# Two layers of a decoder trunk on one core: one block of four small experts moved from the fourth place to the last of 14, and the transposes of the first token tiles moved among the values' products

## The chip, the cores and the metric

The kernel runs on one core of one Trainium2 chip. The metric is device time in microseconds (us) from the first to the last instruction of the core, as the median of several executions. The engines are TensorE (PE in the rows; its weight loads PEld), VectorE (DVE), ScalarE (ACT), GpSimd (POOL), and SyncE (SP), which issues the loads.

## The reference

512 tokens of width 1024 go through two layers and a final norm. Per layer:

```
h  = rms_norm(x)                                   # 512 x 1024
q, k, v, cu, cg, ga, gb = split(h @ w_in)          # 512 wide each, ga and gb 1024
A  = mixture of three dilated windows of attention(q, k, v) @ w_attn_out
B  = silu(layer_norm(depthwise_conv31(cu * sigmoid(cg)))) @ w_conv_out
x += (sigmoid(ga) * A + sigmoid(gb) * B) @ w_out
h2 = rms_norm(x)
group = top-1 of 4;  e1, e2 = top-2 of the group's 8 experts
x += sum over the two experts e: gate_e * ((silu(h2 @ Wg[e]) * (h2 @ Wu[e])) @ Wd[e])
x += sigmoid(rms_norm(x) @ w_ple_gate) * (p @ w_ple_proj)
```

Wg[e] and Wu[e] are 1024 x 512, Wd[e] is 512 x 1024, all in float32; there are 32 experts in each layer.

## The kernel before, in words

**Dense parts.** Tokens are handled in 4 tiles of 128. A float32 product is made of three products of halves: each operand is split into a high part (hi) and the rest (lo), and hi·hi, lo·hi and hi·lo are added (lines 313 to 315). The dense weights lie in chunks of 128x1024; `SEQ_CHUNKS` is their order: v0 to v3 (the values), then cu0, cg0 and so on, pg0 to pg7 last (the gate of the per-layer embeddings). `load_chunks` loads a chunk as s_raw on SP (L217). `split_chunks` makes hi on ACT (L235) and lo: of the four v chunks one half on POOL and one on DVE (L238), of most others the whole 128x1024 on POOL (L240). `take(c)` asks for splits up to chunk c + `self.ahead` and loads up to c + `self.look`.

**The opening of layer 0.** `run` loads the four token tiles and the first chunks. Then it takes the tiles t one after another: the sum of squares on ACT, `prep`, which writes s_n (the normed tile, one operation of 128x1024 on DVE) and appends that tile's `split_T` to the list `self.todo`, and `split_chunks`. `split_T` transposes a tile on TensorE (eight transposes, ps_tr<-s_n, L420), copies the result on ACT (s_hTh, L425) and writes the rest on DVE (s_hTl, L427). In this stretch the program's order on DVE, ACT and POOL is kept as written (`Engines`). Rows of helpers have line 103.

**The values' products.** `tokens_b` calls `token_b` once per token tile: 8 steps k of three products each, ps_tb<-s_hi,s_hTh and its two companions, 96 in all. Chunk v0 serves k = 0 and 1, v1 k = 2 and 3, and so on. `value` copies each tile's result and calls the next `split_T` left in the list. Behind the values stand the chunks of z (ps_z), in steps of 24 products with `step_a`.

**The blocks of experts.** Tokens are sorted to experts with slots. The 28 experts after the first four stand in the order of their load, which is known only after routing: `order_experts` ranks them and gives each a base slot. The eight with the fewest tokens are small (32 slots), the others have 64. `BLK` groups the experts in 14 blocks of 128 slots: two of them each, or four small ones. `moe` takes two blocks per round c: gate and up products of both blocks (ps_g, ps_u), down products of the two blocks of the round before (ps_y), transposes (ps_hT), the gather for the next round (ps_xg), and the combine of the round before (ps_c). After the fifth block stands a loop for tokens that found no slot, at which all queues are drained. In rounds 4 and 5 the projections of the embeddings are added (ps_pe). After the last round the down products of blocks 12 and 13 follow, then their combine (L1150), with transposes of x and the products of the gate behind it.

**The loads of experts.** Weights come in 512 KB tiles, 4 per matrix and expert, in a ring of 45 slots (`s4`, L253). `pump` issues them in the order in which the blocks use them: gate and up of two blocks ahead of the down tiles of the two before, the last down tiles ahead of the raw chunks pg0 to pg7 (L217). SP lets at most eight loads be outstanding: a load is issued when the one eight before it has landed.

Of the kernel before, what the change touches and what calls it, by code (L numbers as in the profile page):

```python
# [13 lines left out]
OP = mybir.AluOpType  # L14
# [5 lines left out]
KD = D // P  # L20
H, HD = 8, 64
CW, CK = 512, 31
NG, NPG, NE = 4, 8, 32
# [3 lines left out]
CAP = 64  # L27
GS = 256


NST, NSM = 4, 8
NDY = NE - NST
LD = 4
BLK = ([(2 * i, 2 * i + 1) for i in range(NST // 2)]
       + [tuple(range(NST + 4 * i, NST + 4 * i + 4)) for i in range(NSM // 4)]
       + [(i, i + 1) for i in range(NST + NSM, NE, 2)])
NB = len(BLK)


# [41 lines left out]
AH = 4  # L81
LK = 5, 3
# [82 lines left out]
class Trunk:  # L165
    def __init__(self, ctx, tc, x, pT, wd, wg, wu, wdn, sm, gains, cst, out):
# [19 lines left out]
        for l in range(self.L):  # L186
            gu = [[(l, w, s, h) for w in ("g", "u") for h in range(4) for s in b
                   if n or w == "u" or h < 4 - LATE] for n, b in enumerate(BLK)]
            dn = [[(l, "d", s, h) for h in range(4) for s in b] for b in BLK]
            seq = gu[:2] + dn[:2]  # L190
# [171 lines left out]
                self.done(c)  # L362
        return ps

    def tokens_b(self, cs, src, then):
        for c in cs:
            self.take(c)
        for t in range(NT):
            then(t, self.token_b(cs, src, t))


    def rsqrt(self, y, a, t, steps=3):
# [63 lines left out]
    def run(self):  # L436
        nc = self.nc
        self.layer = 0
        self.lim = NCH - 1
        nc.sync.dma_start(self.x[0], self.dr["x"][0:P])  # L440
        nc.sync.dma_start(self.ident, self.dr["cst"][:, C_ID:C_ID + P])
        gain = self.gain_row(0)
        for t in range(NT):
            if t:
                nc.sync.dma_start(self.x[t], self.dr["x"][t * P:(t + 1) * P])
            self.load_chunks(t)
        self.small(0)
        self.load_chunks(5)
        self.load_c2()
        nc.sync.dma_start(self.c1[:, C_ID + P:], self.dr["cst"][:, C_ID + P:C_N1])  # L450
        self.oneb = self.one.tile([P, P], BF, name="oneb")
        nc.vector.memset(self.oneb, 1.0)
        self.hT = Rows(self.s4, KD, F32R, "hTh"), Rows(self.s4, KD, F32R, "hTl")
        self.todo = []
        self.nc = Engines(self.tc, ("v", "sc", "g"))
        for t in range(NT):
            n = self.s4.get(F32, "n")
            self.prep(t, gain, self.rms(t, n), n)
            if t in (1, 2):
                self.todo.pop(0)()  # L460
            self.split_chunks(t)
        self.nc = nc
        self.s4.free()
        for l in range(self.L):
            self.layer = l
            self.mixer(l)
            self.moe(l)
            self.ple(l)
# [23 lines left out]
    def mixer(self, l):  # L492
        nc = self.nc
        v, act = nc.vector, nc.scalar
        base = l * NCH
        self.look, self.ahead = LK[0], AH
        pos = self.pos = {s: base + i for i, s in enumerate(SEQ_CHUNKS)}
        self.lim = pos["wo7"]
        conv, attn, side = [], [], []
# [5 lines left out]
        def value(t, ps):  # L505
            act.activation(vt(t), ps, AF.Copy)
            self.ps.free()
            if self.todo:
                self.todo.pop(0)()
        self.tokens_b([pos[f"v{i}"] for i in range(4)], self.hT, value)  # L510

        if l:
            self.load_c2()
        self.scale_small(l)
# [234 lines left out]
        for j in range(8):  # L749
# [14 lines left out]
            for h in range(2):  # L764
# [3 lines left out]
                                       op0=OP.mult, op1=OP.subtract)  # L768
# [17 lines left out]
        cs = [pos[f"wo{i}"] for i in range(4, 8)]  # L786
# [148 lines left out]
    def order_experts(self):  # L935

        v = self.nc.vector
        cnt = self.posb[:, 128:160]
        key, rank, small, base, self.cnt, top, rest, bs = (self.lgT[:, 32 * i:32 * i + 32] for i in range(8))
        bs, ss = bs[:, :8], bs[:, 8:16]  # L940
        over = lambda a, n: a.unsqueeze(1).to_broadcast([P, n, 32])
        down = lambda a, n: a.unsqueeze(2).to_broadcast([P, n, 32])

        v.scalar_tensor_tensor(key, cnt, -32.0, self.cc(C_KEY, 32), op0=OP.mult, op1=OP.add)  # L944
        src = key
        for i in range(0, NE, 8):
            v.max(out=top[:, i:i + 8], in_=src)
            if i + 8 < NE:
                v.match_replace(out=rest, in_to_replace=top[:, i:i + 8], in_values=src, imm_value=-1e9)
                src = rest  # L950
        oi = self.tn(NDY, "oi", I32)
        v.tensor_copy(oi, top[:, :NDY])
        v.tensor_scalar(oi, oi, 31, None, op0=OP.bitwise_and)
        self.order, self.order_v = oi, {}
        tmp = self.s2.get(F32, "ord")
        t3 = tmp.bitcast(BF).rearrange("p (a b) -> p a b", b=32)
        v.tensor_tensor(t3, over(key, 32), down(key, 32), op=OP.is_gt)
        v.tensor_reduce(rank, t3, axis=AX.X, op=OP.add)

        v.tensor_scalar(small, rank, float(NSM), 32.0, op0=OP.is_lt, op1=OP.mult)  # L960
        v.scalar_tensor_tensor(base, rank, float(NSM - 1), small, op0=OP.subtract, op1=OP.mult)
        v.scalar_tensor_tensor(base, rank, float(CAP), base, op0=OP.mult, op1=OP.subtract)
        if CAP * NST != CAP // 2 * NSM:
            v.tensor_scalar(base, base, float(CAP * NST - CAP // 2 * NSM), None, op0=OP.add)
        v.tensor_copy(base[:, :NST], self.cc(C_BASE, NST))
        v.tensor_add(self.cnt, cnt, small)
        self.ps.free()
        E8 = self.Ew[:, 0:256].rearrange("p (g e) -> p g e", e=32)
        t8 = tmp[:, 0:256].rearrange("p (g e) -> p g e", e=32)
        for o, a in ((ss, small), (bs, base)):  # L970
            v.tensor_tensor(t8, E8, over(a, 8), op=OP.mult)
            v.tensor_reduce(o, t8, axis=AX.X, op=OP.add)
        v.tensor_add(self.spos8, self.spos8, ss)
        v.tensor_scalar(ss, self.spos8, float(CAP), 4096.0, op0=OP.is_ge, op1=OP.mult)
        v.tensor_add(ss, ss, bs)
        v.tensor_add(self.slots8, self.spos8, ss)
        self.s2.free()
# [58 lines left out]
    def moe(self, l):  # L1036
# [56 lines left out]
        def gate_up(p, xg, w, ps, hs):  # L1093
            m = P // len(BLK[p])
            for h in hs:
                for k in range(2):
                    for i, e in enumerate(BLK[p]):
                        s = (2 * h + k) % 4 * GS + p % 2 * P + i * m
                        pe.matmul(ps[m * i:m * i + m], xg[h // 2][:, s:s + m], self.half_item((l, w, e, h), k),
                                  start=h == 0 and k == 0, stop=h == 3 and k == 1)  # L1100
                for e in BLK[p]:
                    self.item_free((l, w, e, h))
                self.pump(keep=KEEP[self.c])
# [457 lines left out]
```

## Time and profile before

| What | Value |
| --- | --- |
| time, median of 3 runs | 1854.9 us (1853.12 to 1855.19) |
| the profiled execution's own time | 1849.56 us |
| its span | 1847.8 us |
| TensorE busy | 1750.0 us, 95% |
| DVE, ACT, POOL busy | 47%, 29%, 21% |
| mean granted clock of TensorE | 0.987 |
| moved from memory | 474.90 MB, 258 GB/s over the span |

The profile is of one execution, whose own time lies a little below the median of the runs. Busy shares are averages over stages with different limits. The page's slices show DMA rates of 400 to 419 GB/s in the two stretches of the experts' blocks and some 60 to 80 GB/s in much of the rest. In the rows, `ps_...` are tiles of TensorE's accumulator memory, `s_...` tiles of on-chip memory; the tile written stands ahead of the arrow.

### The profile page before, as it was taken

The numbers are of one execution on the slowest core, as the hardware profiler recorded it, in microseconds if no ns is written. First come the engines' busy times: TensorE is split into PE (matmuls) and PEld (weight loads), VectorE is DVE, ScalarE is ACT, GpSimd is POOL, SyncE is SP. The second block draws the span as 40 slices with busy tenths as digits, with TensorE's granted clock in tenths as the row PEclk, the third lists the DMA queues.
The fourth block names the chain that finished last, engine by engine and source line by source line (L and its number), as shares of the span: only waits on it lengthen the run. The fifth ranks groups of instructions, "written<-read, shape, count | busy, mean of one in ns | idle before, by whom it ended". The sixth has DMA issues, their size and how long they took to land.

```text
span 1847.8 us, 24216 instructions
## 1 busy us (share of the span) xinstructions
PE 1750.0 (95%) x8324; PEld 1055.2 (57%) x8324; DVE 871.8 (47%) x2131; ACT 544.6 (29%) x1041; POOL 379.6 (21%) x203
## 2 busy tenths in 40 slices
PE   5999999989889999999999999999989899999997
PEld 4776777753143455454877777777432443455356
DVE  5587864374041343223558777535620331443146
ACT  4355443321011012112634545342110110121045
POOL 3445332410200001000444443242002000010021
PEclk9999999999999999999999999999999999999999
DMA  5212126479999999997241112554899899999941
GB/s 224 84 65 68 58 79 232 145 264 384 419 359 404 419 419 419 416 419 300 86 133 58 60 57 69 180 195 139 307 391 419 341 418 419 419 414 419 419 197 46
DMA packets 133616, 478.66 MB, mean 259 GB/s; under 512 B 14832, under 2 KB 15344, under 8 KB 133488
## 3 DMA queue, kind: packets, MB, share of 16 engines
q1 hardware_dynamic: 133488, 477.06, 66.4%
q8 instruction: 68, 1.11, 0.2%
q14 instruction: 60, 0.49, 0.1%
HBM read 474.90 MB, written 2.10 MB: 258 GB/s over the span
## 4 chain that ended last, share of the span: by engine, by line
PE 62%; DMA 21%; DVE 8%; issue 5%; ACT 2%; POOL 1%; SPq 0%; POOLq 0%; DVEq 0%; ACTq 0%
DMA s_w<-wdn 11%; PE ps_g L103 8%; PE ps_xg L103 6%; PE ps_u L103 6%; PE ps_z L314 5%; PE ps_z L313 5%; PE ps_z L315 5%; PE ps_y L103 5%; DMA s_w<-wu 5%; PE ps_c L103 5%; DMA s_w<-wg 3%; PE ps_tb L313 2%; PE ps_tb L314 2%; PE ps_tb L315 2%; PE ps_S L634 2%
## 5 line engine op out<-in xcount | busy, mean ns | idle before, releaser
L240 POOL TENSOR_TENSOR s_lo<-s_raw,s_hi 128x1024 fp32r<-128x1024 f32 x114 | 274.8, 2422 | 838.2 <-ACT s_hi L235 464.5
L103 PE MATMUL ps_u<-s_w,s_xg 128*64 128x512 f32 (+1 forms) x1024 | 239.0, 595 | 12.2 <-DMA s_w<-wu 11.8
L103 PE MATMUL ps_g<-s_w,s_xg 128*64 128x512 f32 (+1 forms) x1024 | 225.0, 606 | 14.3 <-DMA s_w<-wdn 9.4
L103 PE MATMUL ps_y<-s_w,s_hT 128*64 128x512 f32 (+1 forms) x1024 | 222.9, 601 | 10.7 <-DMA s_w<-wdn 10.4
L314 PE MATMUL ps_z<-s_hTl,s_hi 128*128 128x512 f32 x512 | 203.9, 398 | 0.0
L313 PE MATMUL ps_z<-s_hTh,s_hi 128*128 128x512 f32 x512 | 201.4, 393 | 0.0
L315 PE MATMUL ps_z<-s_hTh,s_lo 128*128 128x512 f32 x512 | 199.8, 390 | 0.0
L103 PEld LDWEIGHTS ps_u<-s_w,s_xg 128*64 128x64 f32 (+1 forms) x1024 | 67.6, 130 | 178.0 <-issue 118.0
L103 PEld LDWEIGHTS ps_y<-s_w,s_hT 128*64 128x64 f32 (+1 forms) x1024 | 69.2, 131 | 161.7 <-issue 114.3
L103 PEld LDWEIGHTS ps_g<-s_w,s_xg 128*64 128x64 f32 (+1 forms) x1024 | 65.1, 132 | 162.0 <-issue 129.0
L526 DVE SCALAR_TENSOR_TENSOR s_acc<-ps_z,smt,s_acc 128x511 f32<-128x511 f32 (+27 forms) x210 | 153.7, 732 | 4.2
L235 ACT ACTIVATE s_hi<-s_raw 128x1024 fp32r<-128x1024 f32 x120 | 125.4, 1056 | 8.8 <-PE ps_wo L314 4.0
L1108 DVE SCALAR_TENSOR_TENSOR s_h<-s_h,ps_g 128x512 f32<-128x512 f32 x28 | 19.2, 687 | 212.0 <-ACT s_h L1107 194.5
L1107 ACT ACTIVATE s_h<-ps_g,rs 128x512 f32<-128x512 f32 x28 | 19.2, 687 | 328.9 <-PE ps_g L103 327.4
L1153 DVE TENSOR_TENSOR s_x<-s_x,ps_c 128x512 f32<-128x512 f32 x112 | 75.2, 685 | 77.1 <-PE ps_c L103 46.1
L314 PEld LDWEIGHTS ps_z<-s_hTl,s_hi 128*128 128x128 f32 x512 | 96.3, 188 | 21.4 <-issue 3.0
L313 PEld LDWEIGHTS ps_z<-s_hTh,s_hi 128*128 128x128 f32 x512 | 96.1, 188 | 21.3 <-issue 1.0
L103 PE MATMUL ps_xg<-s_OH,s_xh 128*128 128x256 f32 x412 | 104.3, 293 | 3.7 <-DVE s_lgT L944 3.7
L315 PEld LDWEIGHTS ps_z<-s_hTh,s_lo 128*128 128x128 f32 x512 | 96.3, 188 | 19.0
L1118 ACT ACTIVATE s_hT<-ps_hT 128x512 f32<-128x512 f32 x28 | 15.4, 596 | 298.8 <-PE ps_hT L103 298.8
L103 PE MATMUL ps_xg<-s_OH,s_xl 128*128 128x256 f32 x412 | 103.1, 290 | 0.0
L1109 DVE TENSOR_TENSOR s_h<-s_h,ps_u 128x512 f32<-128x512 f32 x28 | 19.2, 687 | 155.2 <-PE ps_u L103 155.2
(274 smaller groups left out, 2815.4 us busy)
## 6 DMA issues: line engine op xcount, KB each, us to landing
s_w<-wu SPq DMA_DIRECT2D x256, 512.0 KB, 9.9
s_w<-wdn SPq DMA_DIRECT2D x256, 512.0 KB, 9.9
s_w<-wg SPq DMA_DIRECT2D x248, 512.0 KB, 9.9
s_raw<-wd SPq DMA_DIRECT2D x124, 512.0 KB, 3.3
s_w<-wg SPq DMA_DIRECT2D x16, 256.0 KB, 7.6
s_x<-x SPq DMA_DIRECT2D x4, 512.0 KB, 9.7
out<-s_n SPq DMA_DIRECT2D x8, 256.0 KB, 2.0
s_gain<-gains SPq DMA_DIRECT2D x3, 512.0 KB, 5.1
```

Of the source, the lines that this page charges most:

```text
L103: i = f(*a, **k)
L235: nc.scalar.activation(hi, raw, AF.Copy)
L240: nc.gpsimd.tensor_tensor(lo, raw, hi.bitcast(F32), op=OP.subtract)
L313: mm(out, lh, rh, start=start, stop=False)
L314: mm(out, lh, rl, start=False, stop=False)
L315: mm(out, ll, rh, start=False, stop=stop)
L526: v.scalar_tensor_tensor(o, i, w, o, op0=OP.mult, op1=OP.add)
L634: nc.tensor.matmul(ps[:, off:off + n], qk(0, i * P, (i + 1) * P)[r], qk(1, 0, n)[r], start=True, stop=True)
L1107: act.activation(t, pg, AF.Tanh, scale=rh[p])
L1108: v.scalar_tensor_tensor(t, t, 1.0, pg, op0=OP.add, op1=OP.mult)
L1109: v.tensor_mul(t, t, pu)
L1153: v.tensor_add(xs, xs, ps)
```

## The change

Blocks: `BLK` had two static pairs, two blocks of four small experts (places 2 and 3), ten pairs. It has now two static pairs, one block of four small experts (place 2), ten pairs, and the other block of four small experts at place 13. The rule for the base slot in `order_experts` follows that. Opening: tile 0's `split_T` runs right after its `prep`; the splits of chunks asked for are 0, 2, 3, 3 instead of 0, 1, 2, 3; the other tiles' `split_T` are called, in layer 0, after the fourth of the eight steps k of a values' tile instead of between tiles or ahead of them; and during the values of layer 0 only one chunk is split ahead instead of four.

```
-BLK = ([(2 * i, 2 * i + 1) for i in range(NST // 2)]
-       + [tuple(range(NST + 4 * i, NST + 4 * i + 4)) for i in range(NSM // 4)]
-       + [(i, i + 1) for i in range(NST + NSM, NE, 2)])
+BLK = ([(2 * i, 2 * i + 1) for i in range(NST // 2)] + [tuple(range(NST, NST + 4))]
+       + [(i, i + 1) for i in range(NST + NSM, NE, 2)] + [tuple(range(NST + 4, NST + NSM))])
...
-    def tokens_b(self, cs, src, then):
+    def tokens_b(self, cs, src, then, hook=None):
         for c in cs:
             self.take(c)
         for t in range(NT):
-            then(t, self.token_b(cs, src, t))
+            then(t, self.token_b(cs, src, t, hook))
...
             self.prep(t, gain, self.rms(t, n), n)
-            if t in (1, 2):
+            self.split_chunks((0, 2, 3, 3)[t])
+            if t == 0:
                 self.todo.pop(0)()
-            self.split_chunks(t)
...
-        self.look, self.ahead = LK[0], AH
+        self.look, self.ahead = LK[0], AH if l else 1
...
-            if self.todo:
+            if l and self.todo:
                 self.todo.pop(0)()
-        self.tokens_b([pos[f"v{i}"] for i in range(4)], self.hT, value)
-
+        halves = []
+
+        def middle():
+            halves.append(0)
+            if not l and len(halves) % KD == KD // 2 and self.todo:
+                self.todo.pop(0)()
+        self.tokens_b([pos[f"v{i}"] for i in range(4)], self.hT, value, middle)
+
+        self.ahead = AH
...
-        v.scalar_tensor_tensor(base, rank, float(NSM - 1), small, op0=OP.subtract, op1=OP.mult)
+
+        v.tensor_scalar(bs32, rank, 4.0, -40.0, op0=OP.is_ge, op1=OP.mult)
+        v.scalar_tensor_tensor(bs32, bs32, -11.0, rank, op0=OP.add, op1=OP.add)
+        v.tensor_mul(base, bs32, small)
         v.scalar_tensor_tensor(base, rank, float(CAP), base, op0=OP.mult, op1=OP.subtract)
-        if CAP * NST != CAP // 2 * NSM:
-            v.tensor_scalar(base, base, float(CAP * NST - CAP // 2 * NSM), None, op0=OP.add)
+        v.tensor_scalar(base, base, -128.0, None, op0=OP.add)
```

On TensorE, at the program's start, before: s_n_108 is token tile 0's normed tile, s_n_131 tile 1's; ps_tr holds transposes, ps_tb_260 the first values' tile.

```order
L420 MATMUL ps_tr_149<-c_71,s_n_108 128x128 x4
L420 MATMUL ps_tr_158<-c_71,s_n_108 128x128 x4
L420 MATMUL ps_tr_190<-c_71,s_n_131 128x128 x4
L420 MATMUL ps_tr_199<-c_71,s_n_131 128x128 x4
L313 MATMUL ps_tb_260<-s_hi_126,s_hTh_100 128x512
L314 MATMUL ps_tb_260<-s_lo_127,s_hTh_100 128x512
```

The same engine in the changed kernel, from step k = 3 of the first values' tile (ps_tb_230); the nine products of k = 0 to 2 stand ahead of it, behind tile 0's own eight transposes, and s_n_149 is tile 1's normed tile.

```order
L313 MATMUL ps_tb_230<-s_hi_167,s_hTh_101 128x512
L420 MATMUL ps_tr_243<-c_71,s_n_149 128x128 x4
L420 MATMUL ps_tr_252<-c_71,s_n_149 128x128
L314 MATMUL ps_tb_230<-s_lo_168,s_hTh_101 128x512
L315 MATMUL ps_tb_230<-s_hi_167,s_hTl_105 128x512
L420 MATMUL ps_tr_252<-c_71,s_n_149 128x128 x3
L313 MATMUL ps_tb_230<-s_hi_172,s_hTh_102 128x512
```

Tile 1's transposes moved from ahead of all products to behind the tenth product of tile 0.

On ACT, later in the opening, before: s_hi_231 is the split of chunk 3, the L235 rows with a 128x1024 tile are splits of later chunks, and ps_tr_286 holds transposes of tile 2, ps_tr_330 of tile 3.

```order
L103 ACTIVATE s_hi_231<-s_raw_86 128x1024
L425 ACTIVATE s_hTh_100<-ps_tr_286 128x2x128
L235 ACTIVATE s_hi_238<-s_raw_89 128x1024
L425 ACTIVATE s_hTh_101<-ps_tr_286 128x2x128
L235 ACTIVATE s_hi_242<-s_raw_91 128x1024
L425 ACTIVATE s_hTh_102<-ps_tr_295 128x2x128
L425 ACTIVATE s_hTh_103<-ps_tr_295 128x2x128
L235 ACTIVATE s_hi_248<-s_raw_246 128x1024
L425 ACTIVATE s_hTh_100<-ps_tr_330 128x2x128
```

The same engine in the changed kernel; ps_tr_252 belongs to tile 1, ps_tr_287 and ps_tr_296 to tile 2, and L508 copies a finished values' tile.

```order
L425 ACTIVATE s_hTh_102<-ps_tr_252 128x2x128
L235 ACTIVATE s_hi_224<-s_raw_89 128x1024
L425 ACTIVATE s_hTh_103<-ps_tr_252 128x2x128
L508 ACTIVATE s_v_218<-ps_tb_230 128x512
L425 ACTIVATE s_hTh_100<-ps_tr_287 128x2x128
L425 ACTIVATE s_hTh_101<-ps_tr_287 128x2x128
L425 ACTIVATE s_hTh_102<-ps_tr_296 128x2x128
L425 ACTIVATE s_hTh_103<-ps_tr_296 128x2x128
L508 ACTIVATE s_v_218<-ps_tb_274 128x512
```

One split of a whole chunk (s_raw_89) stands among the copies now; the next two (s_raw_91 and s_raw_246) have moved behind the values.

On TensorE, at the end of layer 0's blocks, before: the last eight down products of block 13 (ps_y, an expert of 64 slots) and the first of the combine (ps_c).

```order
L103 MATMUL ps_y_6559<-s_w_6381,s_hT_6469 64x512
L103 MATMUL ps_y_6559<-s_w_6383,s_hT_6469 64x512
L103 MATMUL ps_y_6560<-s_w_6381,s_hT_6469 64x512
L103 MATMUL ps_y_6560<-s_w_6383,s_hT_6469 64x512
L103 MATMUL ps_y_6559<-s_w_6389,s_hT_6469 64x512
L103 MATMUL ps_y_6559<-s_w_6391,s_hT_6469 64x512
L103 MATMUL ps_y_6560<-s_w_6389,s_hT_6469 64x512
L103 MATMUL ps_y_6560<-s_w_6391,s_hT_6469 64x512
L1150 MATMUL ps_c_6596<-s_yh_6553,s_OHT_6316 128x512
```

The same place in the changed kernel, where the combine's line is 1162; the expert has 32 slots.

```order
L103 MATMUL ps_y_6546<-s_w_6398,s_hT_6456 32x512
L103 MATMUL ps_y_6546<-s_w_6400,s_hT_6456 32x512
L103 MATMUL ps_y_6546<-s_w_6406,s_hT_6456 32x512
L103 MATMUL ps_y_6546<-s_w_6408,s_hT_6456 32x512
L103 MATMUL ps_y_6547<-s_w_6398,s_hT_6456 32x512
L103 MATMUL ps_y_6547<-s_w_6400,s_hT_6456 32x512
L103 MATMUL ps_y_6547<-s_w_6406,s_hT_6456 32x512
L103 MATMUL ps_y_6547<-s_w_6408,s_hT_6456 32x512
L1162 MATMUL ps_c_6599<-s_yh_6540,s_OHT_6223 128x512
```

The block that stands ahead of the last combine has four experts of 32 slots now, with 16 down tiles instead of 8.

## Rows read from the trace of the kernel before

**Rows 1.** The page's first line.
```profile
span 1847.8 us, 24216 instructions
```
**Rows 2.** Windows, layer 0's blocks: us; busy PE, PEld, DVE, ACT, POOL; PEclk; DMA share; GB/s.
```profile
450.00:505.00 55.00, 48.00 (x178) 8.76 (x178) 2.01 (x4) 0.69 (x1) 6.38 (x3) 1.00 1.03 419
548.00:560.00 12.00, 7.27 (x24) 2.18 (x24) 0.74 (x2) 0.00 (x0) 0.00 (x0) 0.72 0.69 236
780.00:840.00 60.00, 60.00 (x310) 31.83 (x312) 15.26 (x28) 10.42 (x20) 0.00 (x0) 1.00 1.03 419
```
**Rows 3.** Timeline of PE, end of both layers' blocks: start, us, engine, instruction, count.
```profile
855.58 13.95 PE L103 MATMUL ps_y<-s_w,s_hT 128*64 128x512 f32 x64
869.46 0.50 PE L1150 MATMUL ps_c<-s_yh,s_OHT 128*128 128x512 f32 x1
...
1778.85 0.50 PE L1150 MATMUL ps_c<-s_yh,s_OHT 128*128 128x512 f32 x1
```
**Rows 4.** The chain of waits, 580 to 800: start, us, what.
```profile
591.46 1.90 PE ps_y L103 x10
...
725.89 7.28 PE ps_c L103 x32
...
779.96 1.02 PE ps_hT L103 x8
...
788.65 7.28 PE ps_c L103 x32
```
**Rows 5.** Timeline of SP's queue: issue of the eighth raw chunk, both layers.
```profile
857.18 0.33 SPq L217 DMA_DIRECT2D s_raw<-wd  x1
...
1768.81 0.33 SPq L217 DMA_DIRECT2D s_raw<-wd  x1
```
**Rows 6.** Timeline of PE, opening; in brackets idle time before, and its releaser.
```profile
19.21 0.78 PE L313 MATMUL ps_tb<-s_hi,s_hTh 128*128 128x512 f32 x1
...
20.64 0.63 PE L313 MATMUL ps_tb<-s_hi,s_hTh 128*128 128x512 f32 x1
...
24.18 1.03 PE L420 MATMUL ps_tr<-c,s_n 128*128 128x128 f32 x8
...
32.21 0.41 PE L420 MATMUL ps_tr<-c,s_n 128*128 128x128 f32 x2 [0.62 <-DVE s_n L103]
34.87 0.50 PE L314 MATMUL ps_tb<-s_lo,s_hTh 128*128 128x512 f32 x1 [2.25 <-DVE s_lo L103]
...
39.08 0.39 PE L314 MATMUL ps_tb<-s_lo,s_hTh 128*128 128x512 f32 x1
...
49.08 0.39 PE L313 MATMUL ps_z<-s_hTh,s_hi 128*128 128x512 f32 x1
```
**Rows 7.** Timeline of DVE, opening.
```profile
15.34 2.13 DVE L103 SCALAR_TENSOR_TENSOR s_n<-s_x,rms,s_gain 128x1024 f32<-128x1024 f32 x1
17.40 1.40 DVE L103 TENSOR_TENSOR s_hTl<-ps_tr,s_hTh 128x256 fp32r<-128x256 f32 x4
...
24.90 0.68 DVE L103 TENSOR_TENSOR s_lo<-s_raw,s_hi 128x512 fp32r<-128x512 f32 x1
...
29.29 2.77 DVE L103 SCALAR_TENSOR_TENSOR s_n<-s_x,rms,s_gain 128x1024 f32<-128x1024 f32 x1
31.99 2.83 DVE L103 TENSOR_TENSOR s_lo<-s_raw,s_hi 128x512 fp32r<-128x512 f32 x1
```
**Rows 8.** Timeline of POOL, opening.
```profile
15.12 1.27 POOL L103 TENSOR_TENSOR s_lo<-s_raw,s_hi 128x512 fp32r<-128x512 f32 x1 [1.97 <-ACT s_hi L103]
...
26.23 8.04 POOL L240 TENSOR_TENSOR s_lo<-s_raw,s_hi 128x1024 fp32r<-128x1024 f32 x3 [1.34 <-ACT s_hi L235]
```
**Rows 9.** Timeline of ACT, opening: tile 0's copies.
```profile
12.92 1.19 ACT L103 ACTIVATE s_hTh<-ps_tr 128x256 fp32r<-128x256 f32 x4
```
**Rows 10.** Timelines of DVE and PE, layer 0: ordering of experts, first gather after it.
```profile
398.92 0.19 DVE L961 SCALAR_TENSOR_TENSOR s_lgT<-s_lgT 128x32 f32<-128x32 f32 x1
...
428.90 0.36 PE L103 MATMUL ps_xg<-s_OH,s_xh 128*128 128x256 f32 x1
```

More of the change, by code (lines that the diff above doesn't have):

```diff
@@ L445, in run @@
                 nc.sync.dma_start(self.x[t], self.dr["x"][t * P:(t + 1) * P])
-            self.load_chunks(t)
+            if t < 3:
+                self.load_chunks(t)
+        self.load_chunks(3)
         self.small(0)
@@ L939, in order_experts @@
         key, rank, small, base, self.cnt, top, rest, bs = (self.lgT[:, 32 * i:32 * i + 32] for i in range(8))
+        bs32 = rest
         bs, ss = bs[:, :8], bs[:, 8:16]
```

## The prediction, as it was put on record before the run

> **What bounds the kernel now.** The page comes first: its span is 1847.8 us [rows 1], and the profiled execution's own time is 1849.56, 1.8 us more. The median of the runs shown is 1854.9, 5.3 us above that one execution, so I work out differences inside the profiled execution and take them off the median. The share of TensorE (95% busy in the table) says little by itself: a share is an average over stages. I read the two stages that the change touches.
>
> Stage one, the blocks of experts, in the windows. While a block of four small experts runs (450 to 505 us), the DMA engines move 419 GB/s, their share is 1.03, and TensorE is busy 48.00 of 55.00 us: it waits for weights. From 780 to 840 the rate is still 419 GB/s and TensorE is busy 60.00 of 60.00 [rows 2]. Both are full, so the question is which one is behind. A 512 KB tile at 419 GB/s takes 524,288 / 419,000 = 1.25 us. A tile's down products cost TensorE less: the 64 of one pair of blocks (four experts, 16 tiles) take 13.95 us [rows 3], 0.87 us a tile. What lifts pairs over the data is the work beside the tiles: transposes, gather, combine, and in two rounds the embeddings. The combines of two rounds start at 725.89 and 788.65, 62.8 us apart [rows 4], and that round's data is 48 tiles, 60 us. So TensorE falls behind the stream late in the stage, and the end of the stage shows by how much. The last of the eight loads behind the weights is issued at 857.18, and eight loads are outstanding at most, so the last weight tile had landed then; the combine behind the last down products starts at 869.46. That is 12.28 us of TensorE work left with all weights there. In layer 1 it is 1778.85 − 1768.81 = 10.04 [rows 3, 5].
>
> Where TensorE is level with the stream, the end looks otherwise: the chain of waits at 591.46 has 1.90 us of ps_y products behind the landing of a block's last tile [rows 4]. That is after a block of four.
>
> Stage two, the opening of layer 0. The values' first product starts at 19.21, the first product of z at 49.08: 29.87 us [rows 6]. At full speed a product takes (49.08 − 39.08) / 44 = 0.227 us, so 96 take 21.8, and 8.07 are excess. 2.25 of it is a wait for DVE's s_lo, and 0.62 before it one for s_n (the next tile's), together 2.87. Some 2.1 are the transposes of tiles 2 and 3, which stand among the products (1.03 for eight, twice). The other 3.1 is spacing at the lower clock: the first three take 20.64 − 19.21 = 1.43, 0.48 each, twice the later 0.227. Why DVE was late is in its rows: s_n took 2.77 us at 29.29 against 2.13 at 15.34, s_lo 2.83 at 31.99 against 0.68 at 24.90 [rows 7]. Beside them POOL ran three splits of 128x1024 from 26.23 for 8.04 us; its halves take 1.27 [rows 8].
>
> **The change, part by part.**
>
> *The tail of the blocks, per layer.* No byte is added: 28 dynamic experts of 12 tiles, in either order, and the stream is saturated, so the last weight lands when it did. Counted from the end of the sixth round's gate and up, 64 tiles are left before (32 of gate and up, 16 and 16 of down: 80 us) and 88 after (48, 16, 24: 110 us), with the same transposes and combine beside them. TensorE needs 0.87 of each tile's 1.25 us, so it wins 0.38 us a tile. Over the 32 tiles of the four-block's gate and up and the 16 of the down before it, 18 us are won, more than the 10 to 12 that it is behind. The transposes (1.02) and the combine (7.28) then put it 8.3 us behind [rows 4], and the last 24 down tiles win 9.1. That suffices by a margin under 1 us. So the last product ends some 1.90 us behind the last landing, and 12.28 and 10.04 shrink to that: 10.4 + 8.1 = **18.5 us**. Bounds: if the catching up fails by the whole combine, 7.28 stays in each layer and the gain is 3.1 + 0.9 = 4; if not even a product were left behind, it is 22.3. I take 18.5, since the row at 591.46 is this very situation. The raw chunks of the gate for the embeddings come behind the last weight, one per 1.25 us, and are asked for after the first combine; in either order they are last in the queue. I take 0, with 2 us per layer as a bound.
>
> The loop for overflowing tokens after the fifth block drains all queues: 548 to 560 runs at 236 GB/s, 12 × (1 − 236/419) = 5.2 us of stream lost [rows 2]. With one more pair ahead of it TensorE may arrive later; it is level with the stream there, and I take 0, with 5.2 as a bound.
>
> *The opening.* Tile 0's products now start when its own transposes are split, some 13 us (its hTh stand at 12.92 already [rows 9]). Nine of them need chunk 0 and the first half of chunk 1, a tenth only hi; the next meets the second half of chunk 1's lo, which DVE splits behind the s_n of tile 1. That s_n ended at 15.34 + 2.13 = 17.47. Put ahead of it now are tile 0's four hTh on ACT (1.19) and its four hTl on DVE (1.40): between nothing and 2.6 us late, 17.5 to 20.1. I take 1 us, 18.5, because hTl can fill the time in which DVE waits for ACT. From there: 86 × 0.227 = 19.5, transposes of three tiles 3.1, the low clock 3.1 as before: 44.2. The wait of 2.87 goes, because the 128x1024 splits of chunks 5 to 7 no longer run beside DVE (only one is asked for ahead). Gain 49.08 − 44.2 = **4.9 us**. Bounds: 1.9 (the stall alone, less 1 for the later s_n) to 7 (most of the low clock gone). Behind z each step needs one more chunk split, 8.04 / 3 = 2.7 us on POOL against 24 × 0.227 = 5.4 us of products, so the shorter lead is covered; without cover the price is one split, 2.7.
>
> Behind tile 1's sums of squares stand, on ACT, the hi of chunks 1 and 2 at once (each releases a half on POOL), and on DVE the small operations of the norm and then s_n; so POOL's half of chunk 2 comes up about when s_n does, and which is first is open. The row of s_lo (2.83 against 0.68) shows what meeting POOL costs, 1.27 for a half. The Trainium skill ("SBUF — State Buffer", section "Who interferes with whom") says that the two engines share a port under an exclusive lock, so that a two-input operation of DVE waits for POOL's whole instruction; by that rule, if POOL is first, s_n ends 1.3 later and the opening gives 3.6 instead of 4.9. The rows above agree with it.
>
> *DVE in the ordering of experts.* Three more operations of 128x32 per layer at 0.19 us [rows 10]: 0.6. The operations beside which they stand are at 398.92, and the gathers that need the result start at 428.90: some 30 us, of which a few go into the one-hot tiles. Behind that cover 0; without it 0.6 a layer.
>
> Sum: 18.5 + 4.9 = 23.4. The profiled time becomes 1826.2, the median 1854.9 − 23.4 = **1831.5**.
>
> **The rivals.**
>
> *The opening gives nothing* (s_n of tile 1 meets POOL, chunks are late after z): 18.5 alone, 1836.4. For it: every term there hangs on one or two us. Against it: the stall of 2.87 has a visible cause that is moved away. 0.12.
>
> *TensorE's clock falls in the last block.* It waits for each tile there. From 548 to 560, after a wait of several us, the granted clock is 0.72; from 450 to 505, in the same kind of block with a short wait at every tile, it is 1.00 [rows 2]. At the low level (1.2 of 2.4 GHz) a tile's 0.87 becomes 1.74, more than 1.25, and TensorE no longer catches up: over the last 24 tiles it falls 24 × 0.49 = 12 us back, less what full-speed stretches win, since with a backlog it no longer waits. Between 0 and 12 I take 4 per layer, 1839.5. 0.09. [...] The window at 450 speaks against it.
>
> *Slower: the stream itself stops.* The tiles go round a ring of 45 slots. If pairs ahead of the last block fill it, DMA idles and the four-block's extra 30 us of data come late, with nothing behind them to hide it. It decides once the stream idles 23.4 / 2 = 11.7 us more per layer than now: 15 us per layer give 1831.5 + 30 = 1861.5. Against it: 780 to 840 still moves 419 GB/s as the backlog grows to 12 us, ten tiles of 45. 0.03.
>
> *The order of blocks does not come out as written*: it does, as the rows of order above show. *More than forecast* (the low clock of the opening vanishes, no product is left behind): 1826 or less, 0.06.
>
> **How the numbers follow.** The forecast holds 0.70, around 1831.5 with its own bounds 1828 to 1835. The rivals add 0.12 at 1836, 0.09 near 1840, 0.03 above 1854, 0.06 below 1828. The range 1826 to 1842 leaves out the slower case and part of the best one. Faster by over 0.2% (3.7 us, about what a measurement of this kernel can tell from no change) is all but the slower case and the low ends together: 0.94; same 0.03; slower 0.03.
>
> **What would show it.** Right: z starts near 44; no s_n or s_lo of DVE above 2.2 us in the opening; the combine behind the last block starts some 2 us behind the eighth load's issue in both layers; 419 GB/s to the end of the weights; clock 1.00 in the last block. Wrong: a combine that still starts 8 us or more behind it (no catching up), a clock under 0.9 there, a dip in GB/s between 560 and the end of the blocks, or a wait of PE for s_lo behind z.

## The result, and the profile after

The changed kernel takes 1827.88 us (median of 4 runs, 1826.58 to 1830.58) against 1854.01 of before: the ratio is 0.9861, with a 95% interval of 0.9843 to 0.9878, or 25.8 us less (22.6 to 29.1). The forecast was 23.4 less. The profiled execution took 1828.21 us; that of before, 1849.56, lay some 4.5 below its own median, so the two traces differ by only 21.4, and I compare places in them, not their ends.

The page's first line:

```profile
span 1826.4 us, 24223 instructions
```

Three windows of the changed kernel (columns as in [rows 2]); the second is the break between the down products of the round before the last and those of the last.

```profile
780.00:840.00 60.00, 54.50 (x246) 19.31 (x246) 10.30 (x15) 4.09 (x7) 0.00 (x0) 0.97 1.03 419
...
824.80:837.60 12.80, 10.74 (x41) 7.89 (x40) 7.54 (x11) 3.40 (x6) 0.00 (x0) 0.87 1.03 420
829.90:832.50 2.60, 2.60 (x8) 2.01 (x7) 1.35 (x3) 0.00 (x0) 0.00 (x0) 0.50 1.04 424
```

The same stretch that had TensorE busy for 60.00 of 60.00 us has it at 54.50 now (other blocks stand there), with the stream still at 419 GB/s: the bound at the end of the stage has passed to the weights. The timeline of PE at the end of layer 0's blocks, then layer 1's combine:

```profile
824.81 1.09 PE L103 MATMUL ps_hT<-c,s_h 128*128 128x128 f32 x8
827.22 0.49 PE L103 MATMUL ps_c<-s_yh,s_OHT 128*128 128x512 f32 x1 [1.32 <-ACT s_yh L1151]
...
837.63 13.76 PE L103 MATMUL ps_y<-s_w,s_hT 128*64 128x512 f32 x84
851.61 1.05 PE L103 MATMUL ps_y<-s_w,s_hT 128*32 128x512 f32 x2 [0.22 <-DMA s_w<-wdn]
852.86 1.90 PE L103 MATMUL ps_y<-s_w,s_hT 128*32 128x512 f32 x10 [0.20 <-DMA s_w<-wdn]
854.70 0.50 PE L1162 MATMUL ps_c<-s_yh,s_OHT 128*128 128x512 f32 x1
...
1755.89 0.50 PE L1162 MATMUL ps_c<-s_yh,s_OHT 128*128 128x512 f32 x1
```

and SP's queue, the issue of the eighth raw chunk in both layers:

```profile
852.88 0.33 SPq L217 DMA_DIRECT2D s_raw<-wd  x1
...
1754.08 0.33 SPq L217 DMA_DIRECT2D s_raw<-wd  x1
```

The issue marks the landing of the last weight tile: PE's last wait for one ends at 852.86. TensorE's backlog, the work left behind it, is 854.70 − 852.88 = 1.82 us in layer 0 and 1755.89 − 1754.08 = 1.81 in layer 1, where it was 12.28 and 10.04 [rows 3, 5]. The last 1.90 us row is the row that the forecast took from 591.46 [rows 4].

The opening, on PE:

```profile
10.91 0.78 PE L313 MATMUL ps_tb<-s_hi,s_hTh 128*128 128x512 f32 x1
12.05 0.80 PE L314 MATMUL ps_tb<-s_lo,s_hTh 128*128 128x512 f32 x1 [0.36 <-POOL s_lo L103]
...
15.68 0.50 PE L314 MATMUL ps_tb<-s_lo,s_hTh 128*128 128x512 f32 x1 [0.85 <-POOL s_lo L103]
...
18.00 0.77 PE L420 MATMUL ps_tr<-c,s_n 128*128 128x128 f32 x5 [1.38 <-DVE s_n L103]
19.67 0.50 PE L314 MATMUL ps_tb<-s_lo,s_hTh 128*128 128x512 f32 x1 [0.90 <-DVE s_lo L103]
...
20.77 0.77 PE L313 MATMUL ps_tb<-s_hi,s_hTh 128*128 128x512 f32 x1
...
43.23 0.39 PE L313 MATMUL ps_z<-s_hTh,s_hi 128*128 128x512 f32 x1
```

z starts at 43.23 instead of 49.08 [rows 6]. Of these 5.85 us, 1.10 are data that came earlier in this execution: the first s_n of DVE starts at 7.93, and at 9.03 in the trace of before, where it waited for the load of s_gain. I therefore measure z from that s_n: 40.05 us before, 35.30 after, 4.75 less.

### The profile page after: what moved, and what is told of

The parts are those of the page before. It is cut to its first block, busy times and chain, and to the rows that moved or that the text cites. A ratio compares the mean times of both kernels' runs of the same rounds, so it can differ in the third digit from the quotient of the medians.

```text
span 1826.4 us, 24223 instructions
## 1 busy us (share of the span) xinstructions
PE 1737.6 (95%) x8324; PEld 1055.9 (58%) x8324; DVE 869.6 (48%) x2137; ACT 545.1 (30%) x1041; POOL 380.2 (21%) x203
## 4 chain that ended last, share of the span: by engine, by line
PE 67%; DMA 17%; DVE 8%; issue 5%; ACT 2%; POOL 1%; SPq 0%; POOLq 0%; DVEq 0%; ACTq 0%
PE ps_g L103 9%; DMA s_w<-wdn 9%; PE ps_u L103 7%; PE ps_y L103 6%; PE ps_xg L103 6%; PE ps_z L314 6%; PE ps_z L313 6%; PE ps_z L315 6%; DMA s_w<-wu 5%; PE ps_c L103 5%; PE ps_tb L313 2%; PE ps_tb L314 2%; PE ps_tb L315 2%; PE ps_S L643 2%; DMA s_raw<-wd 1%
## 5 line engine op out<-in xcount | busy, mean ns | idle before, releaser
L103 PE MATMUL ps_u<-s_w,s_xg 128*64 128x512 f32 (+1 forms) x1024 | 239.5, 596 | 12.9 <-DMA s_w<-wu 12.6
L103 PE MATMUL ps_g<-s_w,s_xg 128*64 128x512 f32 (+1 forms) x1024 | 207.3, 604 | 9.1 <-DMA s_w<-wdn 8.0
L235 ACT ACTIVATE s_hi<-s_raw 128x1024 fp32r<-128x1024 f32 x120 | 125.1, 1055 | 8.5 <-DMA s_raw<-wd 4.4
L314 PEld LDWEIGHTS ps_z<-s_hTl,s_hi 128*128 128x128 f32 x512 | 96.3, 188 | 21.3 <-issue 3.0
L313 PEld LDWEIGHTS ps_z<-s_hTh,s_hi 128*128 128x128 f32 x512 | 96.1, 188 | 21.3 <-issue 1.0
```

The lines of the kernel that those rows point to most:

```text
L103: i = f(*a, **k)
L235: nc.scalar.activation(hi, raw, AF.Copy)
L313: mm(out, lh, rh, start=start, stop=False)
L314: mm(out, lh, rl, start=False, stop=False)
```

## The experiments

Eleven more kernels ran. "Backlog" is the start of the last combine less the issue of the eighth raw chunk, layer 0 and layer 1; "z" is counted from the first s_n. Times are differences to the kernel before, from the ratio of the runs side by side, with the 95% interval.

| Kernel | Difference, us | Backlog, us | z, us |
| --- | --- | --- | --- |
| before | 0 | 12.28, 10.04 | 40.05 |
| changed | −25.8 (−29.1 to −22.6) | 1.82, 1.81 | 35.30 |
| e1: order of blocks alone | −19.5 (−22.6 to −16.5) | 1.81, 1.82 | 40.10 |
| e2: opening alone | −5.2 (−7.2 to −3.2) | 11.82, 11.00 | 35.21 |
| e3: one chunk ahead alone | −5.7 (−7.8 to −3.9) | 11.27, 11.76 | 35.45 |
| e4: transposes moved, four chunks ahead | −1.9 (−4.4 to +0.9) | 11.55, 10.30 | 37.29 |
| e5: second block of four at place 12 | −22.8 (−26.7 to −18.9) | 1.85, 1.84 | 35.73 |
| e6: both blocks of four last | −25.6 (−28.9 to −22.1) | 1.81, 1.82 | 35.73 |
| e7: before, no embeddings' products | −9.6 (−13.0 to −6.3) | 8.68, 7.95 | 40.45 |
| e8: changed, no embeddings' products | −26.1 (−29.5 to −22.6) | 1.82, 1.82 | 35.71 |
| e9: changed, 7 slots kept free | −24.5 (−27.4 to −21.3) | 1.82, 1.81 | 35.04 |
| e10: order of blocks and one chunk ahead | −26.3 (−29.5 to −23.4) | 1.81, 1.81 | 34.85 |
| e11: changed, last down products twice | −16.5 (−19.7 to −13.5) | 5.61, 3.57 | 35.57 |

**e1, the order of blocks alone.** The edit is the hunks on `BLK` and `order_experts`:

```
+BLK = ([(2 * i, 2 * i + 1) for i in range(NST // 2)] + [tuple(range(NST, NST + 4))]
+       + [(i, i + 1) for i in range(NST + NSM, NE, 2)] + [tuple(range(NST + 4, NST + NSM))])
```

> The new order of blocks alone, opening as before. Theory (TensorE's backlog behind the weights goes, because the block of four is bound by the data): 17 us faster, about 1837; the combine of the last block starts 1.8 us behind the issue of the eighth load in both layers, z starts at 49 as before. Rival (the end of the weights moves later by what TensorE wins, or the opening is what lets it win): under 8 us faster, the combine 2 us behind the eighth load but that load some 8 us later than before.

19.5 us less, the forecast's 18.5. Its timeline of PE, the last combine in both layers (this file's lines stand a few higher):

```profile
860.55 0.50 PE L1152 MATMUL ps_c<-s_yh,s_OHT 128*128 128x512 f32 x1
...
1762.17 0.50 PE L1152 MATMUL ps_c<-s_yh,s_OHT 128*128 128x512 f32 x1
```

and SP's queue, the eighth raw chunk:

```profile
858.74 0.33 SPq L216 DMA_DIRECT2D s_raw<-wd  x1
...
1760.35 0.33 SPq L216 DMA_DIRECT2D s_raw<-wd  x1
```

The backlog is gone with the old opening too, and the eighth chunk is issued at 858.74 against 857.18: 1.56 us later, not some 8, so the stream does not end later by what TensorE wins. The rival falls.

**e2, the opening alone**: the other hunks of the change. One of them, which the excerpt of the change leaves out, loads the fourth token tile ahead of chunk 3; it is in e4 too, and not in e3 and e10.

> The new opening alone, blocks in the order of before. Theory (all that is won at the start is kept to the end, since the stages behind it hang on TensorE): 5 us faster, about 1849, z starts near 43.5 to 44.5. Rival (the start's gain is lost in a later wait, for example for chunks that are split later): z near 44, time within 2 us of before.

5.2 us less, and z 4.84 earlier. What is won at the start is kept, and e1 and e2 add up to 24.7 of the 25.8.

**e3, one chunk split ahead, nothing else of the opening:**

```
-        self.look, self.ahead = LK[0], AH
+        self.look, self.ahead = LK[0], AH if l else 1
...
+        self.ahead = AH
```

> Only one chunk split ahead during the values of layer 0 instead of four, nothing else. Theory of the splits (DVE's s_n and s_lo wait for POOL's 128x1024 splits, and TensorE for DVE): the wait of 2.25 us for s_lo goes, z starts 2 to 3 us earlier, time 2 to 3 us less. Theory of the early start (what counts is that tile 0's products begin before tile 1 is normed): z and time within 1 us of before.

More than either theory: z is 4.60 earlier, as with the whole opening. PE, timeline:

```profile
31.95 0.38 PE L420 MATMUL ps_tr<-c,s_n 128*128 128x128 f32 x2
...
33.09 0.82 PE L420 MATMUL ps_tr<-c,s_n 128*128 128x128 f32 x6
...
44.68 0.39 PE L313 MATMUL ps_z<-s_hTh,s_hi 128*128 128x512 f32 x1
```

From the first product on no wait is left, and the six transposes that took 1.49 us in the kernel before take 0.82. There they stood behind the wait, in this stretch of its timeline of PE:

```profile
35.81 0.63 PE L315 MATMUL ps_tb<-s_hi,s_hTl 128*128 128x512 f32 x1
36.24 1.49 PE L420 MATMUL ps_tr<-c,s_n 128*128 128x128 f32 x6
37.38 0.78 PE L313 MATMUL ps_tb<-s_hi,s_hTh 128*128 128x512 f32 x1
37.95 0.63 PE L314 MATMUL ps_tb<-s_lo,s_hTh 128*128 128x512 f32 x1
38.38 0.63 PE L315 MATMUL ps_tb<-s_hi,s_hTl 128*128 128x512 f32 x1
```

So the wait of 2.87 us drew 1.6 us at the low clock behind it: from 34.87 to 39.08, where the granted clock is 0.59, eight products and six transposes take 4.21 us, and in e3 the same ones take 2.59 (from 32.09 to 34.68, granted clock 1.00). 2.87 + 1.62 = 4.5 of the 4.6.

**e4, the transposes moved and the order of splits and loads, four chunks ahead as before:**

```
-        self.look, self.ahead = LK[0], AH if l else 1
+        self.look, self.ahead = LK[0], AH
```

(a diff against the kernel of e2).

> The moved transposes and the order of splits 0, 2, 3, 3 of the new opening, but four chunks split ahead as before; blocks as before. Theory of the splits: 128x1024 splits on POOL again lie beside the s_n of tiles 2 and 3 and TensorE waits 2 to 3 us for them, so z starts near 46 to 47, 2 to 3 us faster. Theory of the early start: z near 44, 5 us faster, as with the whole new opening.

z is 2.76 earlier, as the theory of the splits had it; the time, 1.9 less, is not clear of no change. Of PE's waits behind tile 1's transposes, this is the long one that e2 does not have; DVE's and POOL's rows beside it follow:

```profile
28.62 0.50 PE L315 MATMUL ps_tb<-s_lo,s_hTh 128*128 128x512 f32 x1 [1.15 <-DVE rms L104]
```

```profile
25.70 2.86 DVE L104 TENSOR_TENSOR s_lo<-s_raw,s_hi 128x512 fp32r<-128x512 f32 x1
```

```profile
22.32 5.70 POOL L241 TENSOR_TENSOR s_lo<-s_raw,s_hi 128x1024 fp32r<-128x1024 f32 x2 [2.10 <-ACT s_hi L236]
```

The s_lo that the product reads takes DVE 2.86 us beside POOL's splits of whole chunks and ends at 28.56 (the releaser in brackets is the profile's guess, a later small operation). DVE is late again while POOL splits whole chunks, with 1.15 us of wait for TensorE, not the 2 to 3 of the expectation.

**e10, the order of blocks with one chunk ahead**, the transposes of the tiles in their old place (the edits of e1 and e3 together).

> The new order of blocks with one chunk split ahead during the values, the transposes of the token tiles where they were before. Theory (in the opening the later splits are worth as much as the whole new opening): the time of the changed kernel within 2 us, 1828. Rival (the moved transposes are worth something beside them): 2 to 4 us slower than the changed kernel, about 1831.

26.3 less: the same as the changed kernel within the intervals, and z is 34.85 against 35.30. The moved transposes bring nothing that shows beside the later splits.

**e7 and e8, no products of the embeddings**, in the kernel before and in the changed one:

```
-            self.step_b(self.pos[f"pe{i}"], pacc, self.pT, 0, True, True)
+            self.take(self.pos[f"pe{i}"])
+            for q in pacc:
+                v.memset(q, 0.0)
+            self.done(self.pos[f"pe{i}"])
```

> The kernel before without the products of the embeddings (192 of them, some 10.9 us of TensorE in each layer, left out; their accumulators are set to 0), blocks in the old order. Theory (TensorE's backlog behind the weights comes from the embeddings and the last combine): the backlog falls from 12.3 and 10.0 us to about 4 in each layer, so 14 us of the 21.8 us of work taken away show: about 1840. Rival (TensorE bounds this stage): 20 us or more, about 1833. Rival (the stage is bound by the weights throughout): under 4 us.

> The changed kernel without the products of the embeddings (left out as in the run before). Theory (with the block of four last the stage is bound by the weights to its end): taking away 21.8 us of TensorE's work gains 0 to 2 us against the changed kernel. Rival (TensorE still bounds a part): 8 us or more.

In the changed kernel 21.8 us less work of TensorE changes the time by 0.3 us, far inside the intervals: the stage hangs on the weights. In the kernel before it gives 9.6 (6.3 to 13.0), between the theory's 14 and the second rival's 4; the sum of backlogs falls by 5.7, not by 14. The timeline of PE in e7, layer 0:

```profile
840.03 1.09 PE L103 MATMUL ps_hT<-c,s_h 128*128 128x128 f32 x8
842.44 0.50 PE L103 MATMUL ps_c<-s_yh,s_OHT 128*128 128x512 f32 x1 [1.31 <-ACT s_yh L1139]
...
852.95 13.95 PE L103 MATMUL ps_y<-s_w,s_hT 128*64 128x512 f32 x64
866.83 0.50 PE L1150 MATMUL ps_c<-s_yh,s_OHT 128*128 128x512 f32 x1
```

TensorE is level with the stream at 840.03: the down products ahead of it still wait for their tiles, 0.17 to 0.18 us each time. Then the transposes and the combine take 852.95 − 840.03 = 12.92 us, not the 8.3 of full speed: the combine waits for ACT's and DVE's copies of the last down result, and the products behind these waits run at the low clock. The 16 tiles that follow win 16 × 0.38 = 6.1, which leaves 12.92 − 6.1 + 1.9 = 8.7, the backlog measured. So the theory is right on where the backlog comes from and wrong in its size, by a break that I took 4.6 too short.

The break does not come from the backlog's being smaller. The kernel before has it too, with TensorE behind the stream; PE's timeline there:

```profile
842.65 1.09 PE L103 MATMUL ps_hT<-c,s_h 128*128 128x128 f32 x8
845.06 0.50 PE L103 MATMUL ps_c<-s_yh,s_OHT 128*128 128x512 f32 x1 [1.31 <-ACT s_yh L1139]
```

Its next down products start at 855.58 [rows 3], 12.93 us behind the transposes.

**e11, each down product of the last block twice.** The changed kernel has the same break, 837.63 − 824.81 = 12.82 us, and 24 tiles at 0.38 win only 9.1. By the working on record 3.7 us should have stayed in each layer beside the 1.9, but the backlog is 1.8. So the narrow products had to be cheaper.

```
-                        pe.matmul(ps[n][m * i:m * i + m], ...,
-                                  ..., start=f == 0, stop=f == 3)
+                        for q in range(1 + (p == NB - 1)):
+                            pe.matmul(ps[n][m * i:m * i + m], ...,
+                                      ..., start=f == 0 and q == 0,
+                                      stop=f == 3 and (q == 1 or p < NB - 1))
```

> The changed kernel with each down product of the last block issued twice (the block's result doubles): a tile of four narrow experts then costs TensorE 0.97 us instead of 0.48, near the 0.87 of a tile of two. Theory (the break for the last transposes and combine but one is 12.8 us, and TensorE catches up only because narrow products take half as long): 8 x 0.38 + 16 x 0.28 = 7.5 us are won against 12.8, so the combine starts some 7 us behind the eighth load instead of 1.8, 10 us slower than the changed kernel in two layers. Rival (the working on record, in which a tile of 0.87 us suffices): backlog under 3 us, within 2 us of the changed kernel.

9.3 us slower than the changed kernel, with 5.61 and 3.57 of backlog: the theory, less its size. 5.61 is the 3.7 + 1.9 of the working on record with the measured break; in layer 1 the break is shorter, 11.32 us with a granted clock of 1.00. The backlogs grow by 5.6 in all; the rest of the 9.3 is within the intervals. PE's timeline in layer 0 (SP issues the eighth chunk at 853.27):

```profile
837.92 21.03 PE L103 MATMUL ps_y<-s_w,s_hT 128*64 128x512 f32 x160
858.88 0.50 PE L1164 MATMUL ps_c<-s_yh,s_OHT 128*128 128x512 f32 x1
```

The row holds 32 products of two experts (32 × 0.218 = 7.0 us) and 128 of four: 14.0 / 128 = 0.11 us each, half of 0.218. A tile of narrow experts costs TensorE some 0.44 us where I wrote 0.87.

**e5 and e6, other places of the narrow blocks.** e5 has the second block of four at place 12 and a pair last, e6 both blocks of four last; `BLK` and the base slots follow, and in e6 the raw chunks are loaded behind `down(NB - 2)`.

```
+       + [(i, i + 1) for i in range(NST + NSM, NE - 2, 2)] + [tuple(range(NST + 4, NST + NSM)), (NE - 2, NE - 1)])
```

> The changed kernel with its second block of four small experts at place 12 and the last pair at 13 (the pair of blocks in the last round changes its order, the bytes stay). Theory (what counts is how many weight tiles are behind the last combine but one, 24 in both, against TensorE's work): same as the changed kernel within 2 us; the combine starts 1 to 3 us behind the eighth load in both layers. Rival (the narrow block must be the last, since its own products make up the time): 5 us or more slower than the changed kernel, about 1833 or more, with 5 us or more behind the eighth load.

> The changed kernel with both blocks of four small experts in the last round (places 12 and 13), ten pairs ahead of them; the raw chunks of the gate are loaded behind the down products of block 12 in the program. Theory: the stream of weights ends as before, the combine 1.8 us behind the landing of the last tile; same as the changed kernel within 3 us, more only if the stream idles. Rival (one block of four early is needed, else the ring of tiles fills and the stream stops in the pairs): the last tile lands 5 us or more later per layer, 10 us slower than the changed kernel.

e6 is the same as the changed kernel; ten pairs without a block of four ahead of them do not stop the stream. In e5 the backlog is 1.85 and 1.84, as the theory has it. Its time is 3 us above the changed kernel's, but the intervals overlap. In its trace the eighth chunk of layer 0 comes 813.83 us behind the first product of z, 4.2 later than in the changed kernel (809.65), and 1.8 of that stands already at the first gather of layer 0; why stays open. PE in e5, layer 0:

```profile
840.91 6.54 PE L103 MATMUL ps_y<-s_w,s_hT 128*32 128x512 f32 x54
...
857.63 1.93 PE L103 MATMUL ps_y<-s_w,s_hT 128*64 128x512 f32 x6 [0.18 <-DMA s_w<-wdn]
859.50 0.50 PE L1163 MATMUL ps_c<-s_yh,s_OHT 128*128 128x512 f32 x1
```

The break there takes 11.31 us, with a granted clock of 1.00. 54 narrow products in 6.54 us, 0.121 each, make up for it; the wide pair behind them runs level with the stream. The narrow block need not be the last, only behind the break.

**e9, 7 slots of the ring kept free** in the round of the overflow loop instead of 9:

```
-KEEP = 3, 6, 9, 6, 6, 6, 3
+KEEP = 3, 6, 7, 6, 6, 6, 3
```

> The changed kernel with 7 instead of 9 slots of the ring kept free in the round of the overflow loop, so that two more tiles can be loaded ahead of it. Theory (the stage is bound by the stream, and the stream stops 6.3 us at that place for a slot that the combine frees): the stop shrinks by up to two tiles, 2.5 us per layer, and all of it shows: 2 to 5 us faster than the changed kernel, about 1824. Rival (the drain of the loop takes back what is loaded earlier, since the queue is empty sooner at the loop): within 1.5 us of the changed kernel.

No gain: 1.3 us above the changed kernel, inside the intervals. A little goes out earlier, and the loop's drain gives back more: from 495 to 515 the stream moves 352 GB/s instead of 345 (0.14 MB more, not the 1 MB of two tiles), from 515 to 545 335 instead of 353 (0.54 MB less). The windows of e9, then those of the changed kernel:

```profile
495.00:515.00 20.00, 20.00 (x114) 13.83 (x114) 12.86 (x28) 4.25 (x10) 0.00 (x0) 1.00 0.93 352
515.00:545.00 30.00, 22.20 (x94) 6.91 (x92) 4.74 (x12) 1.38 (x2) 0.00 (x0) 0.89 0.87 335
```

```profile
495.00:515.00 20.00, 20.00 (x122) 15.03 (x122) 14.05 (x30) 6.14 (x14) 0.00 (x0) 1.00 0.92 345
515.00:545.00 30.00, 26.00 (x122) 8.15 (x122) 5.69 (x14) 1.38 (x2) 0.00 (x0) 0.94 0.92 353
```

No kernel here beats the changed one clearly.

## Why the prediction was right, point by point

**The tail: right in size, and right in its mechanism but for two prices that cancelled.** It said 10.4 + 8.1 = 18.5; the order alone gave 19.5. The backlog fell to 1.82 and 1.81, where 1.90 was forecast. "The transposes (1.02) and the combine (7.28) then put it 8.3 us behind" was 4.5 too short: 12.8. The two rows come from a round in the middle, where the products of the gather stand between them and cover the copies of the down result. The chain of waits of the kernel before has them there:

```profile
780.99 7.67 PE ps_xg L103 x64
```

Behind the down products of the round before the last no gather is left, and the combine waits for the copies, in the kernel before (842.65, under e7) as in the changed one: the right price stood in the trace that the forecast was made from. Without a low clock the break takes 11.3 us (layer 1 of before and e5, granted clock 1.00); in the changed kernel the products behind the waits run at the low clock for some 2.6 us, in layer 0 from 829.90 to 832.50 with a granted clock of 0.50.

"The last 24 down tiles win 9.1" was too little: 8 wide tiles win 8 × 0.38 = 3.0, and 16 narrow ones up to 16 × (1.25 − 0.44) = 13.0. By the right break and the wrong tile 3.7 us a layer would have stayed, and the tail would have been 11 us; e11 comes near to that case. The margin that the text put "under 1 us" is 16.0 − 12.8, about 3. So the 18.5 came out by luck in these two terms.

**The source of the backlog** ("What lifts pairs over the data is the work beside the tiles"): e7 and e8 bear it out. The embeddings made some 3.6 and 2.1 us of it, the last break most of the rest. Of the 9.6 us that e7 gained the backlogs are 5.7; where the other 4 come from stays open (the interval reaches down to 6.3, and the spans of the two traces differ by 5.2).

**The opening: right in size (4.9 forecast, 4.75 in z, 5.2 in time), with the credit in the wrong place and two errors that cancelled.** The sum had the eleventh product at 18.5 and 25.7 us from there to z, with "the low clock 3.1 as before". It starts at 19.67, and with the 1.10 us by which the data came earlier that is 2.3 later than forecast; from there to z are 23.56 us, 2.1 less. Of that 1.5 is the low clock, which costs some 1.6 there: from 19.67 to 23.48, with a granted clock of 0.57, eight products and three transposes take 3.81 us, at the later speed some 2.2. The other 0.6 are five transposes of tile 1, which stand ahead of the eleventh product.

The gain is not that of the early start. e3 and e10 show that the later splits alone give all of it: 2.87 of wait and 1.6 of low clock behind the wait. The early start gives nothing beside that. In the changed kernel twelve products are done when the stretch without waits begins at 20.77, which is 12 × 0.227 = 2.7 us of work; but that is 12.84 after the first s_n, and in e3 the products start 10.3 after it and run without a wait, 2.5 sooner.

**DVE beside POOL.** "No s_n or s_lo of DVE above 2.2 us" was wrong: DVE's timeline, then POOL's, in the changed kernel:

```profile
15.65 2.29 DVE L103 SCALAR_TENSOR_TENSOR s_n<-s_x,rms,s_gain 128x1024 f32<-128x1024 f32 x1
17.87 2.35 DVE L103 TENSOR_TENSOR s_lo<-s_raw,s_hi 128x512 fp32r<-128x512 f32 x2
...
23.09 2.93 DVE L103 SCALAR_TENSOR_TENSOR s_n<-s_x,rms,s_gain 128x1024 f32<-128x1024 f32 x1
...
29.94 1.28 DVE L103 SCALAR_TENSOR_TENSOR s_n<-s_x,rms,s_gain 128x1024 f32<-128x1024 f32 x1
```

```profile
14.34 2.52 POOL L103 TENSOR_TENSOR s_lo<-s_raw,s_hi 128x512 fp32r<-128x512 f32 x2 [2.35 <-ACT s_hi L103]
...
22.56 2.38 POOL L240 TENSOR_TENSOR s_lo<-s_raw,s_hi 128x1024 fp32r<-128x1024 f32 x1 [3.50 <-ACT s_hi L235]
```

At tile 1 the case came that the prediction left open, POOL first: its s_n takes 2.29 us instead of the 1.28 of tile 3, ends (17.94) 1.1 us behind POOL's halves (16.86), and TensorE waits 1.38 us for it at 18.00 and 0.90 for the s_lo behind it at 19.67. It makes the eleventh product late; what the early start would bring without this meeting no run shows. The one whole-chunk split that is left meets the s_n of tile 2, which takes 2.93 us and ends (26.02) 1.1 us behind POOL's (24.94); TensorE has products of tiles 0 and 1 meanwhile and no wait, so this one cost nothing. The Trainium skill ("SBUF — State Buffer", section "Who interferes with whom") has a two-input operation of DVE wait for POOL's whole instruction, and these rows agree.

**The rivals.** "The opening gives nothing" is refuted by e2. "The clock falls in the last block" happened for some 2.6 us in the break (0.50) but not over the stage: 0.97 from 780 to 840, with short waits for tiles all along, and the break (0.87 over 12.8 us) accounts for the missing 0.03. It fell behind the break's waits of 1.32, 0.29 and 0.45 us, yet in e5 it stayed at 1.00 through the same break, so these waits alone do not settle it. The Trainium skill ("TensorE: Matmul & The Clock Gate", section "HAM oscillation — how this bites in real kernels") describes a kernel whose clock is held down because the wait for data in each step is longer than the step's products; the waits of these blocks are far shorter than the products between them, and the clock is not held down. "The stream itself stops": its last weights landed by 852.88 instead of 857.18, with z 5.85 earlier, so some 1.5 us were lost in layer 0, no more than this place differs between kernels with the old order of blocks (808.3 us behind z in e3, 810.6 in e2; here 809.65); in layer 1 none (combine to eighth chunk 899.38 against 899.35). DVE's extra operations in the ordering cannot be told from such differences: the first gather starts 379.8 us behind z in the kernel before, 381.0 in the changed one and 381.3 in e2, which has the old ordering.

**What came back.** In layer 1 the products behind the combine start 22.65 us earlier than in the trace of before (1765.11, 1787.76), and the span ends 21.4 earlier. In the changed kernel the first products of the gate run some 0.43 us apart from 1765.68 to 1767.81, and 0.23 apart in the trace of before; the first seven cost 1.2 us more by it (2.70 against 1.46). That is about the size of these 1.3 us, which were not in the sum.

## What to carry to other kernels

Where a stage is bound by a stream and the engine ends it with a backlog, put last the work that has the most bytes and the least engine time per byte: the engine then ends level with the stream, at no cost in bytes. Take the price of a piece of work from the place where it stands: the transposes and the combine cost 8.3 us in a round where the gather covers the copies, and 11.3 to 12.9 where no gather is left, with a backlog or without one. And test the parts of a change apart even where the sum was right: here the later splits, one part of the edit in the opening, gave all of its gain, and two wrong prices in the tail hid each other.

## What the runs showed of the hardware

A product with 32 columns of weights, four of them side by side on their own rows of one accumulator, takes half the time of one with 64, two side by side: 0.11 to 0.12 us against 0.218, at the same 512 elements moved. The Trainium skill ("TensorEngine Tiling (Array Packing)", section "Tiling Modes") says that the array splits into two parts of 64 columns or four of 32 that work in parallel; these rows agree, and the working on record had one price for both. A wait of 2.87 us in a run of products cost 4.5, since the eight products and six transposes behind it ran at the low clock (granted 0.59). And short waits for tiles, of 0.15 to 0.7 us, left the granted clock at 1.00 for tens of us (450 to 505 in the kernel before; in the changed kernel all of 780 to 840 but the break).
